# Moving one branch projection behind the next gate projection in a two-layer hybrid decoder on one Trainium2 core

## The chip, the cores and the metric

The kernel runs on one core of a Trainium2 chip. The metric is the device time of one execution in microseconds (us). The engines are named as the profile names them: PE is TensorE (PEld its weight loads), DVE is VectorE, ACT is ScalarE, POOL is GpSimd, and SP is SyncE, whose queue (SPq) issues the weight transfers.

## The reference: what is computed

Two layers (`DEPTH = 2`) of a decoder work on 256 tokens of width 1024, in float32. A layer is a token mixer and a SwiGLU, each followed by a LayerNorm. The mixer has three branches that read the same x: A is gated linear attention, B is retention, C is dilated window attention. Each branch gives 512 columns, is projected to 1024 columns, and is weighted by a sigmoid gate of its own:

```python
proj = x @ w_in
(gq, gk, gv, gr, ga, rq, rk, rv, rg, dq, dk, dv, gate) = jnp.split(proj, IN_SPLITS, axis=-1)
...
o_b = _retention_chunked(q_r, k_r, rv.reshape(B, S, N_HEADS, RET_DV))
o_b = _head_group_norm(o_b, ret_norm_g) * jax.nn.silu(rg.astype(F32))
...
y_a = o_a.astype(x.dtype) @ w_branch[0]
y_b = o_b.astype(x.dtype) @ w_branch[1]
y_c = o_c.astype(x.dtype) @ w_branch[2]
gates = jax.nn.sigmoid((gate + b_gate).astype(F32)).reshape(B, S, N_BRANCH, D_MODEL).astype(x.dtype)
merged = gates[:, :, 0] * y_a + gates[:, :, 1] * y_b + gates[:, :, 2] * y_c
return merged @ w_out
```

## The kernel before

**Numbers as two parts.** Every matrix operand is held as a high and a low part, and a product is three matmuls: high by high, low by high, high by low. For a weight, ACT (sometimes DVE, as a CAST) copies the staged block to the high part (`make_hi`, line 196), and DVE subtracts to get the low part (`make_lo`, line 215).

**Weights as a stream.** All weights come as units of 128 by 1024 in the order of use (512 KB each), through six staging buffers. The transfer of a unit is issued when the low part of the unit six places earlier has been made, because that frees its staging buffer. High and low parts live in a ring of 24 blocks (`NR = 24`, tile names `r`), which also holds other things; during the merge at most seven units are held at once (`state["cap"] = (NR - 10) // 2`, line 997). `take(n)` hands out the next units of the stream, `touch(u)` makes sure that both parts are there, and `free(u)` gives the two blocks back.

**The order of the work.** The program is written out by one pass of Python, with each engine's instructions in the order in which they are issued. Attention work runs in generators (`spawn`), which are advanced by one step at each `tick()` between matmul groups, so that it is woven into the dense projections. `await_((l, key))` (line 272) ticks until a generator has issued its last instruction; it is not a wait on the chip, which is done by semaphores.

**The merge (lines 997 to 1040).** For each quarter d of the output columns (256 columns) there are first three gate projections, each of two units and 48 matmuls (`a_pair`, line 408), each followed by a tanh on ACT. Then come three branch projections of one unit and 24 matmuls each, in the order C (`oc`), A (`oa`), B (`ob`). DVE multiplies each by its gate and adds it to the sum `mg`, and ACT and DVE split `mg` into the two parts of `MM`, which the output projection reads after all four quarters.

**What the branch projection reads.** `head_out` (line 871) closes a branch's generator: it transposes the branch's result on PE and lets ACT write the high part `OH` and DVE the low part `OL`, one head of 256 columns at a time. For the retention, `ret_all` (line 767) is issued last of the three; its group norm and its gate run on DVE and POOL before `head_out`.

Matmuls are recorded at line 130, transposes at line 134, ACT, DVE and POOL operations at line 118, and weight transfers at line 138. Rows name tiles without their buffer numbers: `xh`, `xl` are the two parts of x, `r` is a ring block, `pm` and `px` are PSUM banks, `f` are float32 blocks, and `stage` is a staging buffer.

Of the kernel before, what the change touches and what calls it, by code (L numbers as in the profile page):

```python
# [11 lines left out]
AF = mybir.ActivationFunctionType  # L12
OP = mybir.AluOpType
# [41 lines left out]
def trunk(ctx: ExitStack, tc: tile.TileContext, wst, xt_in, x_in, cst, tri, pcol, wga, wa2, lnp, out):  # L55
# [5 lines left out]
    def T(shape, tag, bufs=1, dt=F32):  # L61
        return sb.tile(shape, dt, tag=tag, name=tag, bufs=bufs)
# [11 lines left out]
    def when(log, ap, e):  # L74

        name, a, b = span(ap)
        return max([t + (e != "P" and OWN if by == e else HOP) for x, y, t, by in log.get(name, ()) if x < b and a < y], default=0.0)
# [43 lines left out]
    V = Timed(nc.vector, "V", 1.04, 65)  # L121
    A = Timed(nc.scalar, "A", 0.833, 110)
    G = Timed(nc.gpsimd, "G", 2.1, 450)
    act = A.activation
    stt = V.scalar_tensor_tensor
    ts = V.tensor_scalar

    def mm(out, lhsT, rhs, **k):
        issue("P", [out], [lhsT, rhs], size(out) * (4 if lhsT.dtype == F32 else 1) / 2.4 + 3)
        return nc.tensor.matmul(out, lhsT, rhs, **k)  # L130
# [37 lines left out]
    R = Blocks(sb, NR, 1024, "r", F32R)  # L168
    F4 = Blocks(sb, N4, 1040, "f4")
    F2 = Blocks(sb, N2, 512, "f2")  # L170
    PM = Blocks(psp, 3, 512, "pm")
# [3 lines left out]
    state = {"dma": 0, "made": 0, "whole": 0, "calm": False, "touched": 0, "freed": 0, "cap": NR // 2}  # L175
# [17 lines left out]
    def can_make():  # L193
        return state["made"] - state["freed"] < state["cap"] and len(R.free) >= 2

    def make_hi():
        u = state["made"]
        while state["dma"] <= u:
            dma_next()
        src = staged[u]  # L200
        hi, lo = parts[u] = R.free.pop(0), R.free.pop(0)
        if u in (2, 4, 6):
            start_split(u // 2 + 1)
        for c in halves(u):
            if u == 0:
                start_split(c.start // 512)
            if clk["A"] > clk["V"] + SWITCH:
                V.tensor_copy(hi[:, c], src[:, c])
            else:
                act(hi[:, c], src[:, c], AF.Copy)  # L210
            if u == 0:
                stt(lo[:, c], src[:, c], 1.0, hi[:, c].bitcast(F32), op0=OP.mult, op1=OP.subtract)
        state["made"] += 1

    def make_lo():
        u = state["whole"]
        src = staged.pop(u)
        hi, lo = parts[u]
        for c in halves(u) if u else ():
            stt(lo[:, c], src[:, c], 1.0, hi[:, c].bitcast(F32), op0=OP.mult, op1=OP.subtract)  # L220
        state["whole"] += 1
        if state["dma"] < u + 1 + STAGE:
            dma_next()

    def touch(u):
        state["touched"] = max(state["touched"], u + 1)
        n = 0
        while state["whole"] <= u:
            if state["whole"] < state["made"]:
                make_lo()  # L230
            elif len(R.free) >= 2:
                make_hi()
            else:
                tick()
                n += 1
                assert n < 2000, "ring"
        return parts[u]

    def free(u):
        assert u == state["freed"]  # L240
        R.put(*parts.pop(u))
        state["freed"] += 1

# [6 lines left out]
    def tick():  # L250
        for g in list(side):
            try:
                next(g)
            except StopIteration:
                side.remove(g)

        need = state["touched"] + 2
        late = clk["P"] + (CALM if state["calm"] else BACKLOG)
        if state["whole"] < state["made"]:
            hi = parts[state["whole"]][0]  # L260
            if state["whole"] < need or max(clk["V"], when(written, hi, "V")) < late:
                make_lo()
        if state["made"] < min(total, state["touched"] + AHEAD, state["whole"] + 2) and can_make():
            u = state["made"]
            there = u in staged and when(written, staged[u], "A") < clk["P"] + READY
            if u < need or there and min(clk["A"], clk["V"] - SWITCH) < late:
                make_hi()

    done = set()
    OT = {}  # L270

    def await_(*keys):
        left = 3000
        while not all(k in done for k in keys):
            tick()
            left -= 1
            assert left, keys
# [51 lines left out]
    hcol = T([128, L, 32], "hcol")  # L329
# [68 lines left out]
    def b_group(units, lh, ll, tt, ps, dl=1, last=False):  # L398

        n = len(units)  # L400
        for i, u in enumerate(units):
            b_unit(u, i, n, lh, ll, tt, ps, dl)
            if last:
                free(u)
            if i < n - 1:
                tick()

    def a_pair(units, rh, rl, ps):

        n = len(units)  # L410
        for a in range(2):
            for i, u in enumerate(units):
                hi, lo = touch(u)
                for j in range(4):
                    k = 4 * i + j
                    c0 = j * 256 + a * 128
                    o = ps[:, a * 256:a * 256 + 256]
                    mm(o, hi[:, c0:c0 + 128], rh(k), start=(i == 0 and j == 0), stop=False)
                    mm(o, hi[:, c0:c0 + 128], rl(k), start=False, stop=False)
                    mm(o, lo[:, c0:c0 + 128], rh(k), start=False, stop=(i == n - 1 and j == 3))  # L420
                if a == 1:
                    free(u)
                if not (a == 1 and i == n - 1):
                    tick()
# [3 lines left out]
    def take(n):  # L428
        r = list(range(base[0], base[0] + n))
        base[0] += n  # L430
        return r
# [466 lines left out]
    for l in range(L):  # L898
# [34 lines left out]
        us = take(8)  # L933
# [26 lines left out]
        for g in range(3):  # L960
# [3 lines left out]
            for which in range(2):  # L964
                for hp in range(2):
                    us = take(2)
                    ps = PM.main()[0]
# [28 lines left out]

        state["cap"] = (NR - 10) // 2
        MM = []
        for d in range(4):
            tg = []  # L1000
            for br in range(3):
                us = take(2)
                ps = PM.main()[0]
                a_pair(us, xh, xl, ps)
                t = F2.main()[0]
                for a in range(2):
                    c = br * 8 + d * 2 + a
                    act(t[:, a * 256:a * 256 + 256], ps[:, a * 256:a * 256 + 256], AF.Tanh,
                        bias=hcol[:, l, c:c + 1], scale=0.5)
                PM.put(ps)  # L1010
                tg.append(t)
                tick()
            mg = F2.main()[0]
            for br, key in ((2, "oc"), (0, "oa"), (1, "ob")):
                await_((l, key))
                OH, OL = OT[l, key]
                us = take(1)
                ps = PM.main()[0]
                a_pair(us, lambda k: OH[:, k * 256:k * 256 + 256], lambda k: OL[:, k * 256:k * 256 + 256], ps)
                if br == 2:  # L1020
                    stt(mg, tg[br], 1.0, ps, op0=OP.add, op1=OP.mult)
                else:
                    stt(tg[br], tg[br], 1.0, ps, op0=OP.add, op1=OP.mult)
                    V.tensor_add(mg, mg, tg[br])
                PM.put(ps)
                F2.put(tg[br])
                tick()
                if d == 3:
                    R.put(OH, OL)
            if d % 2 == 0:  # L1030
                MM.append(R.main(2))
            c = slice((d % 2) * 512, (d % 2) * 512 + 512)
            mh = MM[-1][0][:, c]
            act(mh, mg, AF.Copy, scale=0.5)
            stt(MM[-1][1][:, c], mg, 0.5, mh.bitcast(F32), op0=OP.mult, op1=OP.subtract)
            F2.put(mg)


        state["cap"] = (NR - 4) // 2
        ln1 = ln_params(l, 0)  # L1040
        us = take(8)
        for tt in range(2):
            st = T([128, 2, 6], "lnst", 2)
            for c in range(2):
                ps = PM.main()[0]
# [74 lines left out]
        for p in range(NPAIR):  # L1120
# [3 lines left out]
            t = F2.main()[0]  # L1124
# [199 lines left out]
```

## Time and profile before

| | |
|---|---|
| median of 3 runs | 1059.21 us (1058.38 to 1059.3) |
| the profiled execution's own time | 1059.59 us |
| its span (first to last instruction) | 1057.8 us |
| PE busy, share of the span | 1040.2 us, 98% |
| PEld / DVE / ACT / POOL busy | 954.2 / 695.7 / 485.5 / 17.9 us |
| mean granted TensorE clock | 0.995 of full speed |
| moved by DMA | 192.25 MB, 182 GB/s on the mean |

Busy times overlap, since the engines run side by side. A matmul's recorded duration overlaps with the next one's, so that a stretch of matmuls is measured from start to start. [...]

### The profile page before, as it was taken

What the parts mean: (1) busy time and instruction counts of PE and PEld (TensorE: products, weight loads), DVE (VectorE), ACT (ScalarE), POOL (GpSimd) and SP (SyncE); (2) the same over time, 40 slices, a digit from 0 to 9 for tenths busy, and PEclk for the clock granted to TensorE, in tenths of its full rate; (3) what the DMA queues carried; (4) which work ended last, traced back from release to release, by engine and by line L of the source; (5) the groups of instructions that cost most, each with busy time, mean ns of one, the idle gap of its engine ahead of it and who ended that gap; (6) DMA issues with size and microseconds to landing.
All of it is one profiled execution on the core that took longest, in us unless ns stands there. A gap on an engine that the chain in (4) does not pass through costs nothing.

```text
span 1057.8 us, 17494 instructions
## 1 busy us (share of the span) xinstructions
PE 1040.2 (98%) x7122; PEld 954.2 (90%) x7122; DVE 695.7 (66%) x1066; ACT 485.5 (46%) x733; POOL 17.9 (2%) x24
## 2 busy tenths in 40 slices
PE   8999999999999999999999999999899999999997
PEld 6999988898998899999889999878899988999996
DVE  6687765775658755454688767477666686555454
ACT  6565554543444444344364554654433545444330
POOL 0000000000000000000000000000000000000000
PEclk9999999999999999999999999999999999999999
DMA  9686633445666675555376456344456667665521
GB/s 340 231 276 196 204 114 123 141 140 187 191 173 216 191 257 180 192 195 190 120 275 201 143 167 204 106 134 139 131 178 192 193 197 248 206 199 176 192 91 40
DMA packets 55666, 192.25 MB, mean 182 GB/s; under 512 B 6257, under 2 KB 7409, under 8 KB 55586
## 3 DMA queue, kind: packets, MB, share of 16 engines
q1 hardware_dynamic: 50400, 180.38, 52.2%
q10 hardware_dynamic: 5186, 10.76, 3.1%
q8 instruction: 56, 0.92, 0.4%
q14 instruction: 24, 0.20, 0.1%
HBM read 187.93 MB, written 3.18 MB: 181 GB/s over the span
## 4 chain that ended last, share of the span: by engine, by line
PE 94%; DVE 3%; DMA 1%; POOL 1%; issue 1%; ACT 0%; SPq 0%; DVEq 0%
PE pm L130 75%; PE px L130 17%; PE px L134 2%; DVE r L118 1%; DVE f L118 1%; DMA stage<-in_wst_dram 1%; POOL rrs L118 0%; DVE rst L118 0%; ACT r L118 0%; SPq L138 0%; DVE xres L118 0%; POOL grs L118 0%; ACT junk L118 0%; DVE rmv L118 0%; DVE rve L118 0%
## 5 line engine op out<-in xcount | busy, mean ns | idle before, releaser
L130 PE MATMUL pm<-xh,r 128*128 128x256 f32 x2688 | 481.0, 280 | 0.0
L118 DVE SCALAR_TENSOR_TENSOR r<-stage,r 128x1024 fp32r<-128x1024 f32 (+1 forms) x341 | 402.0, 1215 | 50.9 <-ACT r L118 48.9
L130 PEld LDWEIGHTS pm<-xh,r 128*128 128x128 f32 x2688 | 414.1, 189 | 1.2
L118 ACT ACTIVATE r<-stage 128x1024 fp32r<-128x1024 f32 (+1 forms) x327 | 332.8, 1051 | 96.8 <-PE pm L130 35.0
L130 PE MATMUL pm<-xl,r 128*128 128x256 f32 x1344 | 375.3, 279 | 0.0
L130 PEld LDWEIGHTS pm<-xl,r 128*128 128x128 f32 x1344 | 253.2, 188 | 0.9
L130 PE MATMUL pm<-r,xh 128*128 128x512 f32 x672 | 214.9, 400 | 1.5 <-ACT r L118 0.9
L130 PEld LDWEIGHTS pm<-r,xh 128*128 128x128 f32 x672 | 123.5, 190 | 28.9 <-DVE r L118 1.8
L130 PE MATMUL pm<-r,xl 128*128 128x512 f32 x336 | 131.9, 393 | 0.0
L130 PE MATMUL pm<-r,r 128*128 128x256 f32 (+1 forms) x768 | 121.4, 317 | 6.5 <-DVE r L118 5.9
L130 PEld LDWEIGHTS pm<-r,r 128*128 128x128 f32 x768 | 108.8, 195 | 16.2 <-DVE r L118 8.1
L130 PE MATMUL px<-r,r 128*128 128x512 f32 x528 | 122.6, 389 | 0.0
L130 PEld LDWEIGHTS px<-r,r 128*128 128x128 f32 x528 | 97.9, 188 | 19.3
L118 DVE SCALAR_TENSOR_TENSOR f<-f,pm 128x512 f32<-128x512 f32 x52 | 35.7, 686 | 114.0 <-ACT f L118 93.7
L118 ACT ACTIVATE f<-pm 128x512 f32<-128x512 f32 x72 | 42.7, 594 | 141.9 <-PE pm L130 140.3
L130 PEld LDWEIGHTS pm<-r,xl 128*128 128x128 f32 x336 | 63.7, 190 | 13.8
L118 ACT ACTIVATE r<-f 128x512 fp32r<-128x512 f32 x28 | 17.7, 632 | 97.2 <-DVE f L118 97.2
L130 PE MATMUL px<-f,f 128*128 128x128 f32 (+4 forms) x368 | 47.4, 292 | 0.0
L130 PEld LDWEIGHTS px<-f,f 128*128 128x128 f32 (+2 forms) x368 | 42.7, 184 | 4.0 <-issue 0.7
L118 ACT ACTIVATE f<-px 128x512 f32<-128x512 f32 (+2 forms) x52 | 25.2, 506 | 41.2 <-PE px L130 29.2
L118 ACT ACTIVATE f<-pm,hcol 128x256 f32<-128x256 f32 x48 | 20.2, 474 | 51.1 <-PE pm L130 51.1
L118 DVE TENSOR_TENSOR f<-f,pm 128x512 f32<-128x512 f32 x22 | 15.1, 688 | 40.9 <-PE pm L130 40.7
(102 smaller groups left out, 485.9 us busy)
## 6 DMA issues: line engine op xcount, KB each, us to landing
stage<-in_wst_dram SPq DMA_DIRECT2D x339, 512.0 KB, 4.5
f<-in_lnp_dram ACTq DMA_DIRECT2D x8, 512.0 KB, 7.5
scr<-f ACTq DMA_DIRECT2D x8, 260.0 KB, 3.6
f<-scr ACTq DMA_DIRECT2D x4, 520.0 KB, 4.4
xres<-in_x_dram ACTq DMA_DIRECT2D x4, 256.0 KB, 5.5
out_dram<-xres SPq DMA_DIRECT2D x4, 256.0 KB, 2.0
f<-in_xt_dram SPq DMA_DIRECT2D x3, 256.0 KB, 8.6
cst<-in_cst_dram ACTq DMA_DIRECT2D x4, 192.0 KB, 3.2
```

Of the source, the lines that this page charges most:

```text
L118: return f(*a, **k)
L130: return nc.tensor.matmul(out, lhsT, rhs, **k)
L134: return nc.tensor.transpose(out, in_, ident)
```

## The change

In the first quarter (d = 0) of each layer, the retention's branch projection, its multiply and add, and the split of the first quarter's sum are no longer issued in their place. They are issued after the first gate projection of the second quarter (d = 1). The weight unit of the moved projection is still taken from the stream in its old place; two later units are given back before it, so the assertion that units come back in order is dropped.

```diff
     def free(u):
-        assert u == state["freed"]
         R.put(*parts.pop(u))
         state["freed"] += 1
...
+        late = None
+        for d in range(4):
+            tg = []
+            for br in range(3):
+                tg.append(merge_gate(d, br))
+                if late:
+                    branch(*late[1])
+                    merged(late[0], late[1][-1])
+                    late = None
+            mg = F2.main()[0]
+            for br, key in ((2, "oc"), (0, "oa"), (1, "ob")):
+                us = take(1)
+                if d == 0 and br == 1:
+                    late = d, (us, br, key, tg[br], mg)
+                else:
+                    branch(us, br, key, tg[br], mg)
+                if d == 3:
+                    R.put(*OT[l, key])
+            if not late:
+                merged(d, mg)
```

`merge_gate`, `branch` and `merged` hold the old loop's body, line by line.

The first place is PE in layer 0, at the end of the first quarter's projection of branch A (`r_83`, `r_84` are A's two parts, `r_82`, `r_73` its weights). Here `px_113<-cst,f_95` are the last four transposes of the retention's result, `r_76`, `r_77` are its `OH` and `OL`, `r_85`, `r_86` the weight unit of its projection, and `r_87`, `r_88`, `r_65`, `r_66` the two units of the next gate. Before:

```order
L130 MATMUL pm_107<-r_83,r_73 128x256
L134 MATMUL px_113<-cst,f_95 128x128 x4
L130 MATMUL pm_106<-r_76,r_85 128x256 [waits Activation_49]
L130 MATMUL pm_106<-r_77,r_85 128x256 [waits DVE_49]
L130 MATMUL pm_106<-r_76,r_86 128x256
...
L130 MATMUL pm_108<-xh,r_87 128x256
L130 MATMUL pm_108<-xl,r_87 128x256
L130 MATMUL pm_108<-xh,r_88 128x256
```

With the change:

```order
L134 MATMUL px_113<-cst,f_95 128x128 x4
L130 MATMUL pm_106<-xh,r_87 128x256 [waits Activation_49]
L130 MATMUL pm_106<-xl,r_87 128x256
L130 MATMUL pm_106<-xh,r_88 128x256
...
L130 MATMUL pm_106<-xh,r_66 128x256 [waits DVE_49]
...
L130 MATMUL pm_108<-r_76,r_85 128x256 [waits DVE_49,Activation_49]
L130 MATMUL pm_108<-r_77,r_85 128x256 [waits DVE_49]
L130 MATMUL pm_108<-r_76,r_86 128x256
```

The 24 matmuls of the retention's projection and the 48 of the gate have changed places; the transposes stand where they stood. Layer 1 shows the same exchange.

The second place is DVE in layer 0, from the split of the gate's second unit (`r_66`) on. `r_77<-px` are the low parts `OL`, two heads to a row, `f_105<-f_105,pm` is the multiply behind the retention's projection, and `r<-stage,r` are low parts of weight units. Before:

```order
L118 SCALAR_TENSOR_TENSOR r_66<-stage,r_65 128x1024 [waits DMAHW0_49,Activation_49]
...
L118 SCALAR_TENSOR_TENSOR r_77<-px_113,hcol,r_76 128x256 [waits Activation_49] x2
L118 SCALAR_TENSOR_TENSOR r_79<-stage,r_78 128x1024 [waits DMAHW4_49,Activation_49]
L118 SCALAR_TENSOR_TENSOR f_105<-f_105,pm_106 128x512 [waits PE_49]
L118 TENSOR_TENSOR f_102<-f_102,f_105 128x512 [waits DVE_49]
L118 SCALAR_TENSOR_TENSOR r_73<-f_102,r_82 128x512 [waits Activation_49]
L118 SCALAR_TENSOR_TENSOR r_81<-stage,r_80 128x1024 [waits DMAHW5_49]
L118 SCALAR_TENSOR_TENSOR r_86<-stage,r_85 128x1024 [waits DMAHW6_49,Activation_49]
```

With the change:

```order
L118 SCALAR_TENSOR_TENSOR r_66<-stage,r_65 128x1024 [waits DMAHW0_49,Activation_49]
...
L118 SCALAR_TENSOR_TENSOR r_77<-px_113,hcol,r_76 128x256 [waits Activation_49] x2
L118 SCALAR_TENSOR_TENSOR r_79<-stage,r_78 128x1024 [waits DMAHW4_49,Activation_49]
L118 SCALAR_TENSOR_TENSOR r_81<-stage,r_80 128x1024 [waits DMAHW5_49,Activation_49]
L118 SCALAR_TENSOR_TENSOR r_73<-stage,r_82 128x1024 [waits DMAHW6_49,Activation_49]
L118 SCALAR_TENSOR_TENSOR f_105<-f_105,pm_108 128x512 [waits PE_49]
L118 TENSOR_TENSOR f_102<-f_102,f_105 128x512 [waits DVE_49]
L118 SCALAR_TENSOR_TENSOR r_66<-f_102,r_65 128x512 [waits Activation_49]
```

Everything up to the last `OL` is as before; then two weight splits stand ahead of the multiply, the add and the split of the sum, where they stood behind them. On ACT, one weight copy per layer is added that was a CAST on DVE, and the rest keeps its kind and count; SP issues the same transfers in the same order.

## Rows read from the trace of the kernel before

**Rows 1.** The page's first part: busy time, share of the span, instructions.

```profile
PE 1040.2 (98%) x7122; PEld 954.2 (90%) x7122; DVE 695.7 (66%) x1066; ACT 485.5 (46%) x733; POOL 17.9 (2%) x24
```

**Rows 2.** The waits of PE: us in total, times, longest us.

```profile
PE pm L130 <- DVE r L118: 6.5, 6, 2.2
PE px L130 <- DVE f L118: 2.2, 3, 1.5
```

**Rows 3.** Timeline of PE, layer 0: start, us, what, idle before it.

```profile
235.30 0.36 PE L130 MATMUL pm<-r,r 128*128 128x256 f32 x1
236.44 1.64 PE L130 MATMUL pm<-r,r 128*128 128x256 f32 x6 [0.77 <-DVE r L118]
240.31 4.38 PE L130 MATMUL pm<-r,r 128*128 128x256 f32 x17 [2.23 <-DVE r L118]
244.50 0.38 PE L130 MATMUL pm<-xh,r 128*128 128x256 f32 x1
...
261.56 8.69 PE L130 MATMUL pm<-r,r 128*128 128x256 f32 x71
```

**Rows 4.** Timeline of PE, the same place in layer 1.

```profile
757.85 0.36 PE L130 MATMUL pm<-r,r 128*128 128x256 f32 x1
...
762.79 4.34 PE L130 MATMUL pm<-r,r 128*128 128x256 f32 x17 [2.23 <-DVE r L118]
766.97 0.28 PE L130 MATMUL pm<-xh,r 128*128 128x256 f32 x1
```

**Rows 5.** Windows, PE alone: length, PE busy (count), PEclk, DMA share, GB/s.

```profile
238.00:240.00 2.00, 0.08 (x1) 1.00 0.97 293
240.00:242.00 2.00, 1.54 (x6) 0.83 0.54 217
242.00:244.00 2.00, 2.00 (x11) 0.50 0.18 10
246.00:248.00 2.00, 2.00 (x19) 1.00 0.04 16
```

**Rows 6.** Timeline of DVE, layer 0.

```profile
231.90 3.49 DVE L118 SCALAR_TENSOR_TENSOR r<-stage,r 128x1024 fp32r<-128x1024 f32 x3
...
240.80 0.48 DVE L118 SCALAR_TENSOR_TENSOR r<-px,hcol,r 128x256 fp32r<-128x256 f32 x1 [0.54 <-ACT r L118]
241.75 1.23 DVE L118 SCALAR_TENSOR_TENSOR r<-stage,r 128x1024 fp32r<-128x1024 f32 x1 [0.46 <-ACT r L118]
244.74 0.69 DVE L118 SCALAR_TENSOR_TENSOR f<-f,pm 128x512 f32<-128x512 f32 x1 [1.76 <-PE pm L130]
...
247.52 2.35 DVE L118 SCALAR_TENSOR_TENSOR r<-stage,r 128x1024 fp32r<-128x1024 f32 x2
```

**Rows 7.** Timeline of DVE, layer 1.

```profile
754.39 3.49 DVE L118 SCALAR_TENSOR_TENSOR r<-stage,r 128x1024 fp32r<-128x1024 f32 x3
...
763.28 0.48 DVE L118 SCALAR_TENSOR_TENSOR r<-px,hcol,r 128x256 fp32r<-128x256 f32 x1 [0.54 <-ACT r L118]
```

**Rows 8.** Timeline of ACT, layer 0.

```profile
240.67 1.99 ACT L118 ACTIVATE r<-stage 128x1024 fp32r<-128x1024 f32 x2
...
250.46 0.84 ACT L118 ACTIVATE f<-pm,hcol 128x256 f32<-128x256 f32 x2 [2.62 <-PE pm L130]
...
256.11 0.84 ACT L118 ACTIVATE f<-pm,hcol 128x256 f32<-128x256 f32 x2 [2.92 <-PE pm L130]
```

**Rows 9.** A short stop of PE in layer 0 (timeline).

```profile
202.79 0.71 PE L130 MATMUL px<-f 64*128 64x128 f32 x6 [0.36 <-DVE f L118]
```

**Rows 10.** Window round the first stop: us; PE, PEld, DVE, ACT, POOL busy; PEclk, DMA, GB/s.

```profile
196.00:206.00 10.00, 9.64 (x72) 7.79 (x71) 5.08 (x13) 5.59 (x20) 2.03 (x2) 1.00 0.62 210
```

**Rows 11.** What the weight supply waits for: SPq and ACT, whole run.

```profile
SPq L138 <- DVE r L118: 847.4, 328, 15.5
...
ACT r L118 <- PE pm L130: 35.0, 26, 3.4
```

**Rows 12.** DMA issues: KB each, median us from issue to landing.

```profile
stage<-in_wst_dram SPq DMA_DIRECT2D x339, 512.0 KB, 4.5
```

More of the change, by code (lines that the diff above doesn't have):

```diff
@@ L998, in trunk, with merge_gate, branch, merged @@
         MM = []
[L999 to L1029, printed above, removed]
+        def merge_gate(d, br):
+            us = take(2)
+            ps = PM.main()[0]
+            a_pair(us, xh, xl, ps)
+            t = F2.main()[0]
+            for a in range(2):
+                c = br * 8 + d * 2 + a
+                act(t[:, a * 256:a * 256 + 256], ps[:, a * 256:a * 256 + 256], AF.Tanh,
+                    bias=hcol[:, l, c:c + 1], scale=0.5)
+            PM.put(ps)
+            tick()
+            return t
+        def branch(us, br, key, t, mg):
+            await_((l, key))
+            OH, OL = OT[l, key]
+            ps = PM.main()[0]
+            a_pair(us, lambda k: OH[:, k * 256:k * 256 + 256], lambda k: OL[:, k * 256:k * 256 + 256], ps)
+            if br == 2:
+                stt(mg, t, 1.0, ps, op0=OP.add, op1=OP.mult)
+            else:
+                stt(t, t, 1.0, ps, op0=OP.add, op1=OP.mult)
+                V.tensor_add(mg, mg, t)
+            PM.put(ps)
+            F2.put(t)
+            tick()
+        def merged(d, mg):
             if d % 2 == 0:
@@ L1036, in trunk @@
             F2.put(mg)
+        late = None
[12 more added lines that the diff above has]
+                    late = d, (us, br, key, tg[br], mg)
+                else:
+                    branch(us, br, key, tg[br], mg)
[3 more added lines that the diff above has]
+                merged(d, mg)
         state["cap"] = (NR - 4) // 2
```

## The prediction

> **What bounds the kernel now.** I read the page first. PE is busy for 98% of the span, DVE for 66% and ACT for 46% [rows 1], so only a stretch in which PE stands still, or runs slowly, can be worth anything. The second view is PE's own waits. They come to little: 6.5 us of matmuls behind DVE's writes to ring blocks in six waits, 2.2 us the longest, and 2.2 us in three waits at the attention's small products [rows 2]. The third view, PE's timeline, shows where the long ones lie. In layer 0 the first matmul of the retention's projection starts at 235.30. PE then stands still for 0.77 us, does six matmuls, stands still for 2.23 us, and does the other 17 in 4.38 us; the next gate starts at 244.50 [rows 3]. Layer 1 does the same from 757.85 to 766.97 [rows 4]. DVE's timeline says for what PE waits: the last of the retention's low parts (`OL`) is begun at 240.80 and lasts 0.48 us [rows 6], so it is there at 241.28; in layer 1 at 763.76 [rows 7]. DVE comes to them late because the retention's group norm runs through it and three weight splits stand ahead (231.90, 3.49 us) [rows 6].
>
> The windows add a second cost that the waits don't show. The granted clock is 1.00 while PE has almost nothing to do (238 to 240), 0.83 over the next two us, 0.50 from 242 to 244, where PE is busy all the time, and 1.00 again from 246 [rows 5]. [...] So the 17 matmuls after the stop run at half speed, and the stop costs more than its idle time.
>
> **What the stop costs.** The same work without a stop: the three branch projections of the second quarter are 72 matmuls in a row, of which 71 have records, from 261.56 for 8.69 us [rows 3]. Less the 0.2 us by which the last one's record outlasts the step to the next, that is 8.5 us, or 2.8 us for 24. In layer 0 they took 244.50 - 235.30 = 9.2 us, which loses 6.4 us; in layer 1 766.97 - 757.85 = 9.1 us, which loses 6.3 us [rows 3, 4]. Of the 6.4 us, 0.77 + 2.23 = 3.0 are idle; the last 17 take 244.50 - 240.31 = 4.2 us where 17 x 2.8/24 = 2.0 would do, so 2.2 are the slow clock; and the remaining 1.2 are the first seven matmuls, which take 0.36 + 1.64 us for 0.8, held up head by head.
>
> **The change part by part.** *Nothing is removed.* PE issues the same matmuls; 48 of the gate come ahead of 24 of the branch. The transposes that feed `OH` and `OL` stand where they stood, and DVE's order up to the last `OL` is word for word the same, so I let that last `OL` end at 241.28 and 763.76 as before. It waits for no matmul that is moved.
>
> *The gate moved forward.* Its length is the distance from one gate's tanh to the next in the second quarter: 256.11 - 250.46 = 5.65 us, or 0.118 us for each of its 48 matmuls [rows 8]. It would begin at 235.30 and end at 240.95. Does it have its weights? Its first unit was split before the retention's norm; the low part of its second unit is the first of the three splits at 231.90 and so is there at 233.1 [rows 6]. Its first use is the fifteenth matmul, 14 x 0.118 = 1.6 us behind the start, at 236.9: 3.8 us to spare. In layer 1 the split ends at 755.6 and the use is at 759.5 [rows 4, 7]. So the gate doesn't wait.
>
> *The branch moved back.* It starts at 240.95. Its heads come in order, and the last one's low part is read by the eleventh matmul, ten steps of 0.118 us later, at 242.1, against 241.28. That is 0.8 us to spare. In layer 1 it is 757.85 + 5.65 + 1.2 = 764.7 against 763.76, 0.9 us. So the wait is covered, but with a margin of under 1 us, and this is the tightest place of the forecast. With PE busy throughout, there is nothing left that would take the clock down here: the stretch from 196 to 206 holds a stop of 0.36 us, with the clock at 1.00 [rows 9, 10].
>
> *DVE and ACT behind it.* Two splits now stand ahead of the branch's multiply. The first of them follows the split at 241.75, which ends at 242.98 [rows 6]; its high part is the second ACT copy of the pair at 240.67, done at 242.66 [rows 8]. So it ends at 244.2. The second needs a high part that ACT can copy only after the gate's tanh (0.84 us) and its own 1.0 us, at 244.5, and ends at 245.7. The multiply then starts at 245.7 and not at the branch's end, 243.8. Its PSUM bank is wanted next by the second quarter's first branch projection, at 240.95 + 2.8 + 2 x 5.65 = 255.05: nine us of cover, so I cost the 1.9 us at nothing; without that cover it would cost 1.9 us per layer. The split of the sum is read by the output projection alone, after three more quarters. The CAST that becomes an ACT copy takes 1.05 us per layer on an engine that is 46% busy. The weight transfers keep their order and number.
>
> **The sum.** 1059.59 - 6.4 - 6.3 = 1046.9 us for an execution like the profiled one, which lies 0.4 us above the runs' median. I say 1046.7.
>
> **Rivals.**
>
> *The wait only becomes shorter.* If DVE's chain ends x us later than before, PE waits x - 0.8 us. For it speaks the small margin, and that DVE then works beside a PE that is busy rather than idle. Against it, the operations in question have waits on ACT and POOL, none on moved work. Nothing in the rows gives x. Its bounds are 0 and the 2.23 us of the old stop; at 2.2 the wait is 1.4 us, and if the clock falls again another 2.2 us at most, 3.6 us per layer: 1047 to 1054 us. Still faster.
>
> *PE runs ahead and finds its weights late, so that the gain is given back.* PE comes 6.4 us earlier to everything behind. The second quarter's first branch unit has its low part at 248.7 (two splits from 247.52) and is used at 261.56, a lead of 12.9 us [rows 3, 6]. After the change I have 244.2 against 255.05, a lead of 10.8. Against it: SPq spends 847 us in 328 waits for DVE's splits, and ACT waits 35 us for PE to release blocks, so the stream stands at its ring's limit and not at the memory's [rows 11]. The likeliest place for a late unit is the second of the two splits that now stand ahead of the multiply: while it waits for its transfer, so do the multiply and everything behind it on DVE. A unit takes 4.5 us to land [rows 12], and this one's transfer is issued when the first of the splits at 231.90 ends, at 233.1, so it lands near 238, and ACT wants it at 243.5: it would have to be 11 us later still before PE's next branch, at 255.05, waited. [...] If part or all of the lead were lost, the time would be anything from 1047 up to 1059.6.
>
> *The ring runs dry and the kernel is slower.* The old order gave the branch's unit back at its end, one after the other. Now it is held for a gate longer (5.65 us), with at most seven units in the ring. If a new unit can only start when one comes back, each costs a transfer (4.5 us), a copy (1.0) and a split (1.2) in a row, 6.7 us, where PE uses one in 2.8 us: 3.9 us lost per unit. It decides against the change from the point at which the lead of 10.8 us is used up; from then on two late units per layer lose 7.8 us and more than eat the 6.4 us, and at three the time is 1059.6 - 12.7 + 6 x 3.9 = 1070 us. Against it speaks that the gate ahead gives two units back at 240.95, 3 us before the held one comes due.
>
> That the change doesn't do what it says is excluded by the order of PE's rows: the swap is there in both layers, and nowhere else.
>
> **How the numbers follow.** I give the forecast 0.86, the shortened wait 0.06, the weights running late 0.05 (of which 0.02 within 0.2% of before) and the ring 0.03. 0.2% (2 us) is about what a measurement of this kernel can tell from no change. So faster is 0.86 + 0.06 + 0.03 = 0.95, same 0.02, slower 0.03. For the range I take the likeliest case and part of the first rival. PE's other waits in the old kernel, 2.2 us at the small products [rows 2], are the most that a shifted order could also take away, so the low end is 1045.0; the upper end leaves room for a rest wait of 1 us per layer, 1049.0. Beyond it lie most of the first rival and the other two, 0.12 together.
>
> **What would show it right or wrong.** Right: PE's waits behind DVE's ring blocks fall from 6.5 us to under 1; the granted clock stays at 1.00 between 235 and 250; the gate starts near 235.3 and the branch takes 2.8 us from about 241; the second gate starts near 243.8 and its rest is 6.4 us earlier than before, and 12.7 us earlier behind layer 1's merge. DVE's multiply starts near 245.7, with no one waiting. Wrong: a stop of PE at the branch's seventh to eleventh matmul with a clock of 0.50 behind it (the first rival), or PE waiting for `r<-stage` at the later gates (the other two). The span would tell the rest: a shortened merge but an unchanged span would mean that the gain is given back in the feed-forward part.

## The result, and the profile after

The changed kernel's median is 1046.89 us (four runs, 1044.9 to 1048.09) against 1059.26 us (four runs, 1058.38 to 1059.53): a ratio of 0.9883 with a 95% interval of 0.9865 to 0.99. 1046.7 us was forecast. The profiled execution took 1048.09 us, with a span of 1046.2 us.

The page's first part after the change answers to [rows 1]:

```profile
PE 1034.1 (99%) x7122; PEld 950.7 (91%) x7122; DVE 693.9 (66%) x1064; ACT 487.2 (47%) x735; POOL 17.9 (2%) x24
```

PE's waits answer to [rows 2] (us in total, times, longest us):

```profile
PE pm L130 <- ACT r L118: 2.4, 1, 2.4
PE px L130 <- DVE f L118: 2.2, 3, 1.5
```

The line of 6.5 us behind DVE's ring blocks is gone. PE's busy time is 6.1 us shorter although it does the same matmuls; a part of that is the half clock: in the windows, 11 matmuls are busy for 2 us at 0.50 [rows 5] and 19 at 1.00 (below). In the list there is now one wait of 2.4 us for ACT, which lies elsewhere (below). The timeline of PE in layer 0, which answers to [rows 3]:

```profile
237.57 0.60 PE L134 MATMUL px<-cst,f 128*128 128x128 f32 x4
237.92 0.36 PE L130 MATMUL pm<-xh,r 128*128 128x256 f32 x1
...
243.66 3.04 PE L130 MATMUL pm<-r,r 128*128 128x256 f32 x24
246.54 0.28 PE L130 MATMUL pm<-xh,r 128*128 128x256 f32 x1
```

The gate follows the transposes at once and lasts 5.74 us; the retention's projection follows without a stop and takes 2.88 us. From the gate's start to the next gate's start are 8.62 us. Before, the projection began at 235.30 [rows 3], and the next gate but one, whose first matmul is the second of this row, began at 250.25:

```profile
250.14 0.40 PE L130 MATMUL pm<-xh,r 128*128 128x256 f32 x2
```

That is 14.95 us for the same 72 matmuls, so the change saves 6.33 us here. In layer 1 the same stretch takes 8.61 us instead of 14.78 us and saves 6.17 us. The windows, which answer to [rows 5], show the granted clock (PEclk) in shares of full speed:

```profile
240.00:242.00 2.00, 2.00 (x19) 1.00 0.96 326
242.00:244.00 2.00, 2.00 (x19) 1.00 0.78 229
```

DVE in the same place, as in [rows 6]:

```profile
243.43 0.49 DVE L118 SCALAR_TENSOR_TENSOR r<-px,hcol,r 128x256 fp32r<-128x256 f32 x1 [0.54 <-ACT r L118]
244.38 2.36 DVE L118 SCALAR_TENSOR_TENSOR r<-stage,r 128x1024 fp32r<-128x1024 f32 x2 [0.46 <-ACT r L118]
247.00 1.23 DVE L118 SCALAR_TENSOR_TENSOR r<-stage,r 128x1024 fp32r<-128x1024 f32 x1 [0.26 <-ACT r L118]
248.14 0.68 DVE L118 SCALAR_TENSOR_TENSOR f<-f,pm 128x512 f32<-128x512 f32 x1
```

The whole program stands 2.62 us later here than before (237.92 against 235.30). Less that, the last low part is begun at 240.81 (240.80 before) and the multiply at 245.5 (245.7 was forecast): up to the last low part DVE has not moved, PE has.

A measure that leaves the rest of the program out is the distance on ACT from the tanh behind the first quarter's third gate to the tanh behind the third quarter's first gate, with the same matmuls in between in both kernels. Below it is called *the distance*. Before, in layer 0, it is 275.86 - 228.98 = 46.88 us:

```profile
228.98 0.84 ACT L118 ACTIVATE f<-pm,hcol 128x256 f32<-128x256 f32 x2 [5.40 <-PE pm L130]
...
275.86 0.84 ACT L118 ACTIVATE f<-pm,hcol 128x256 f32<-128x256 f32 x2 [2.42 <-PE pm L130]
```

After, it is 271.72 - 231.60 = 40.12 us:

```profile
231.60 0.84 ACT L118 ACTIVATE f<-pm,hcol 128x256 f32<-128x256 f32 x2 [5.40 <-PE pm L130]
...
271.72 0.84 ACT L118 ACTIVATE f<-pm,hcol 128x256 f32<-128x256 f32 x2 [2.43 <-PE pm L130]
```

Layer 1 has 46.71 and 40.11 us. So the two merges are 6.76 and 6.60 us shorter, 13.4 us in sum: 12.5 us at the old stop, and 0.43 us per layer in the second and third gates of the second quarter, which took 5.65 us each before [rows 8] and take 5.44 us now. The spans differ by 1057.8 - 1046.2 = 11.6 us. The rest lies in two other places. 2.62 us are lost in the first 60 us of this execution, 1.8 of them in the first 16 us. And layer 1's first stretch gains 0.8 us. -13.36 + 2.62 - 0.83 = -11.57. Two of these pieces stand in the chain of work (start, us, engine and line, matmuls). Before:

```profile
30.07 30.18 PE pm L130 x228
536.64 44.75 PE pm L130 x288
```

After:

```profile
31.86 31.01 PE pm L130 x228
532.51 43.94 PE pm L130 x288
```

The same 228 matmuls lose 0.83 us and the same 288 gain 0.81 us, without a wait. In both kernels three matmuls of 256 columns took 340 or 353 ns from start to start (the last experiments), and these two stretches and the two gates changed from the one to the other.

### The profile page after: what moved, and what is told of

Read it like the earlier page. It is cut to its first block, busy times and chain, and to the rows that moved or that the text cites. A ratio compares the mean times of both kernels' runs of the same rounds, so it can differ in the third digit from the quotient of the medians.

```text
span 1046.2 us, 17496 instructions
## 1 busy us (share of the span) xinstructions
PE 1034.1 (99%) x7122; PEld 950.7 (91%) x7122; DVE 693.9 (66%) x1064; ACT 487.2 (47%) x735; POOL 17.9 (2%) x24
## 4 chain that ended last, share of the span: by engine, by line
PE 98%; DMA 1%; DVE 1%; issue 0%; ACT 0%; POOL 0%; SPq 0%; DVEq 0%
PE pm L130 78%; PE px L130 18%; PE px L134 2%; DMA stage<-in_wst_dram 1%; DVE xres L118 0%; POOL grs L118 0%; DVE f L118 0%; ACT junk L118 0%; SPq L138 0%; DVE lnst L118 0%; DVEq L1338 0%; ACT r L118 0%; DVE gss L118 0%; DVE mv L118 0%; DVE ve L118 0%
## 5 line engine op out<-in xcount | busy, mean ns | idle before, releaser
L118 ACT ACTIVATE r<-stage 128x1024 fp32r<-128x1024 f32 (+1 forms) x329 | 334.8, 1052 | 96.6 <-PE pm L130 39.9
L130 PE MATMUL pm<-r,r 128*128 128x256 f32 (+1 forms) x768 | 115.2, 310 | 0.0
L130 PEld LDWEIGHTS pm<-r,r 128*128 128x128 f32 x768 | 105.3, 190 | 7.3
```

Of the source, the lines that this page charges most:

```text
L118: return f(*a, **k)
```

## The experiments

Times and ratios are against the kernel before in the same series. Two theories are told apart throughout. Mine is that PE stopped, once per layer, for the retention's late low parts, that the stop took the clock down too, and that one gate covers it whole. Against it stand the rivals of the forecast (a margin that doesn't hold, weights that come late, a ring that runs dry) and that the gain is something of the whole program.

**The change in one layer (layer0).**

```diff
-                if d == 0 and br == 1:
+                if l == 0 and d == 0 and br == 1:
                     late = d, (us, br, key, tg[br], mg)
```

> The change in layer 0 alone, layer 1 as before. My theory (a stop of TensorE that is the same in each layer is taken away): layer 0's merge is shortened by the 6.8 us that the changed kernel shows there, layer 1's stop from its retention projection stays at 9.1 us with the clock at 0.50 behind it; time 1059.2 - 6.8 = 1052.4 us, ratio about 0.9935. Rival (the gain is one of the whole program, by the order in which ring blocks come back): layer 1 gains too, or layer 0 gains another amount than 6.8 us.

1052.0 us, ratio 0.9935 (0.9919 to 0.995). The distance is 40.12 us in layer 0 and 46.83 us in layer 1. Layer 1's timeline of PE still has the stop:

```profile
750.76 1.65 PE L130 MATMUL pm<-r,r 128*128 128x256 f32 x6 [0.73 <-DVE r L118]
754.64 4.39 PE L130 MATMUL pm<-r,r 128*128 128x256 f32 x17 [2.23 <-DVE r L118]
```

The second idle time is that of [rows 4]; the first was 0.71 us in the kernel before:

```profile
758.92 1.64 PE L130 MATMUL pm<-r,r 128*128 128x256 f32 x6 [0.71 <-DVE r L118]
```

The gain is local, and half of it belongs to each layer. That layer 1 is as long as before hides two differences that nearly cancel. The half clock lasts longer here and reaches into the next gate, which starts at 758.83:

```profile
758.00:760.00 2.00, 2.00 (x11) 0.50 0.82 231
```

And the second and third gates take 5.44 us each instead of 5.65 us, although this layer has PE's old order.

**The splits behind the low parts, PE's order as before (hold).** The flag is set in `ret_all` behind the last gate multiply, and cleared at the end of `head_out`.

```diff
+            state["hold"] = tt == 1
...
+        state["hold"] = False
...
-        if state["whole"] < state["made"]:
+        if state["whole"] < state["made"] and not state["hold"]:
             hi = parts[state["whole"]][0]
```

> TensorE's order as before; instead no weight split is issued on VectorE between the retention's last gate multiply and its last low part, so that the splits that stood ahead of the low parts stand behind them. My theory (the low parts were late because VectorE had 3.5 us of splits and one more of 1.2 us ahead of them): the last low part comes at about 238.5 instead of 241.3, TensorE stops for about 2 us instead of 3, in two pieces, and the projection takes 5 us instead of 9.2 if the clock stays up, 6.5 if it falls; time 1050.5 to 1054. Rival (the low parts wait for the group norm and the transposes, and the splits only fill its gaps): the projection still takes 8 us or more; time 1057 or more.

1051.58 us, ratio 0.9929 (0.9904 to 0.9955). The distance is 41.94 us in layer 0 and 43.50 us in layer 1. PE's timeline, layer 0 and then layer 1:

```profile
237.88 1.19 PE L130 MATMUL pm<-r,r 128*128 128x256 f32 x7
240.08 2.96 PE L130 MATMUL pm<-r,r 128*128 128x256 f32 x17 [1.01 <-DVE r L118]
242.88 0.29 PE L130 MATMUL pm<-xh,r 128*128 128x256 f32 x1
...
754.65 1.20 PE L130 MATMUL pm<-r,r 128*128 128x256 f32 x7
756.86 3.96 PE L130 MATMUL pm<-r,r 128*128 128x256 f32 x17 [1.01 <-DVE r L118]
760.62 0.41 PE L130 MATMUL pm<-xh,r 128*128 128x256 f32 x1
```

The projection took 5.0 us in layer 0, as expected with the clock up. The last low part is begun 9.01 us behind the tanh instead of 11.82 us. So the splits in DVE's order were what made the low parts late: with them moved, half of the gain and more comes without touching PE's order. Layer 1 shows the same stop, to the hundredth, and yet 17 matmuls that take 1.0 us longer. The windows say why:

```profile
240.00:242.00 2.00, 1.77 (x10) 1.00 0.00 0
242.00:244.00 2.00, 2.00 (x19) 1.00 0.34 74
...
758.00:760.00 2.00, 2.00 (x12) 0.61 0.07 4
760.00:762.00 2.00, 2.00 (x11) 0.54 0.92 264
```

The same stop of 1.01 us left the clock at 1.00 in the one layer and was followed by windows at 0.61 and 0.54 in the other. Layer 0 also tells what the half clock cost in the kernel before: its last 17 matmuls take 242.88 - 240.08 = 2.8 us at a clock of 1.00, still held up by the last low part, where the old ones took 4.2 us [rows 3]. That is 1.4 us.

**Filling the stop with work that is thrown away (fill).**

```diff
                 ps = PM.main()[0]
+                if d == 0 and br == 1:
+                    for _ in range(36):
+                        mm(ps[:, 0:256], touch(us[0])[0][:, 0:128], xh(0), start=True, stop=True)
```

> TensorE's order as before, with 36 matmuls of 256 columns added ahead of the first quarter's retention projection in each layer; their sums are thrown away. They take 36 x 0.1175 = 4.2 us, which is nearly the stop. My theory (of the 6.4 us lost per layer some 2 are the half clock that the stop brings): the clock stays at 1.00, the last low part still comes at 241.3, the projection ends near 243.1 instead of 244.5; time 1059.2 - 2 x 1.4 = 1056.4 us. Rival (the clock's fall is not brought by the stop, or costs nothing): the projection ends at 244.5 or later as before, time 1059.2 or more.

1055.42 us, ratio 0.9962 (0.9949 to 0.9975), a little better than expected. The distances are 44.76 and 44.73 us, 2.1 and 2.0 us shorter than before.

```profile
236.85 4.49 PE L130 MATMUL pm<-xh,r 128*128 128x256 f32 x36
241.17 3.66 PE L130 MATMUL pm<-r,r 128*128 128x256 f32 x24
244.67 0.29 PE L130 MATMUL pm<-xh,r 128*128 128x256 f32 x1
```

The kernel stands 1.55 us later here than before (230.53 against 228.98 at the tanh), so the projection ends at 243.1 in the old kernel's time, not at 244.5. The clock is 1.00 in every window from 234 to 248. A kernel with 72 matmuls more is faster: the half clock behind the stop is a cost of its own, 1.4 us here, as in hold, and it is gone with the 36 matmuls in the stop. The other 0.7 us per layer are the three gates behind it, which go faster (below).

**Behind two gates instead of one (two_gates).**

```diff
-                if late:
+                if late and br == 1:
                     branch(*late[1])
```

> As the changed kernel, but the retention's projection stands behind two gates of the second quarter instead of one. My theory (one gate covers the wait whole, with 0.8 us to spare): no further gain, 1046.9 us within 1.5 us. Rival (the margin is too small in some executions, or the cover is not whole): 1 us or more faster than the changed kernel; or, if holding the unit longer starves the ring, slower.

1046.6 us, ratio 0.9878 (0.9861 to 0.9895), the same as the changed kernel's. The distances are 40.34 and 40.32 us, 0.2 us longer; the two gates ahead of the projection take 11.39 us together, so the second of them has not gone to the faster step. One gate (5.74 us) was cover enough, and holding the unit for another gate cost no more than these 0.2 us per layer.

**The retention's low parts made later (late1, late4, late8).** The same edit with 1, 4 and 8 operations, on the changed kernel:

```diff
+            if key == "ob" and hp == 0:
+                for _ in range(4):
+                    nc.vector.scalar_tensor_tensor(OL[:, 0:512], o[:, 0:512], 1.0, o[:, 512:1024],
+                                                   op0=OP.mult, op1=OP.subtract)
             if col is None:
```

> As the changed kernel, with one more VectorE operation of 0.7 us ahead of the retention's first low part in each layer (it writes values that are overwritten). My theory (0.8 us of margin): still no stop at the projection; from the tanh behind the first quarter's third gate to the tanh behind the third quarter's first gate 40.1 us, as in the changed kernel. Rival (no margin, each delay of VectorE comes through): 40.8 us.

> As the changed kernel, with four such operations (2.8 us) ahead of the retention's first low part in each layer. My theory (0.8 us of margin): TensorE stops for about 2.0 us in all at the projection; the same distance is 42.1 us if the clock stays at 1.00, up to 44.3 if it falls to half. Rival (more margin than I think, or none): 40.1, or 42.9 us and more with the clock at 1.00.

> As the changed kernel, with eight such operations (5.5 us) ahead of the retention's first low part in each layer. My theory: a stop of about 4.7 us, the clock falls to 0.50 behind it, and the distance is 45 to 47 us, nearly the 46.9 us of the kernel before. Rival (the clock does not fall, since TensorE was busy up to the stop): 44.8 us with the clock at 1.00.

Measured, with the distance in us (the start of the last low part is counted from the same tanh, 11.83 us in the changed kernel):

| | last low part later by | distance, layers 0 and 1 | more than the changed kernel | lowest granted clock in the merge |
|---|---|---|---|---|
| changed kernel | - | 40.12, 40.11 | - | 1.00 |
| late1 | 0.80 | 40.13, 40.12 | 0.01 | 1.00 |
| late4 | 2.99 | 42.31, 42.25 | 2.2 | 1.00 |
| late8 | 5.89 | 47.65, 47.40 | 7.5, 7.3 | 0.50 |

late4's last low part is begun at 243.16, 14.82 us behind its tanh at 228.34; late8's at 247.07, 17.72 us behind 229.35; late1's 12.63 us behind its tanh. So late1 is free and late4 costs 2.2 us of its 3.0: the margin is 0.8 us, as forecast. late8 would cost 5.9 - 0.8 = 5.1 us by the wait alone, and costs 2.4 us more (2.2 us in layer 1). Its timeline of PE in layer 0, and behind it the windows:

```profile
242.71 1.65 PE L130 MATMUL pm<-r,r 128*128 128x256 f32 x6 [1.01 <-DVE r L118]
246.59 4.38 PE L130 MATMUL pm<-r,r 128*128 128x256 f32 x17 [2.23 <-DVE r L118]
```

```profile
248.00:250.00 2.00, 2.00 (x11) 0.50 0.03 8
250.00:252.00 2.00, 2.00 (x11) 0.50 0.73 231
252.00:254.00 2.00, 2.00 (x16) 0.75 0.97 324
```

This is the old stop, moved behind the gate: the same 17 matmuls in 4.38 us. Here the half clock outlasts them by some 2 us and slows the next gate too, which is why it costs more than the 1.4 us of the kernel before. late4's timeline has a stop too, but in its windows the clock stays at 1.00:

```profile
242.67 2.97 PE L130 MATMUL pm<-r,r 128*128 128x256 f32 x17 [1.27 <-DVE r L118]
```

```profile
242.00:244.00 2.00, 1.19 (x5) 1.00 0.87 250
244.00:246.00 2.00, 2.00 (x19) 1.00 0.03 8
```

**The changed kernel once more (again).** No edit.

> The changed kernel once more, in more rounds: its four times lay between 1044.9 and 1048.1 us. My theory (the spread comes from the first 50 us, where the profiled execution lost 2.6 us that the change has nothing to do with): the time stays near 1046.5 us, and an execution without that loss in its first 50 us spans about 1043.5 us. Rival (the spread comes from the merge, where the margin is under 1 us): a slower execution shows a stop at the retention's projection.

1045.84 us (1044.89 to 1045.96), ratio 0.9862 (0.9838 to 0.9886). The profiled execution spans 1044.1 us and has the distance 40.12 us in both layers, with the clock at 1.00 from 228 to 248. The first tanh of the measure is at 229.47 instead of 231.60. So the 2.1 us by which the two profiled executions differ arose before the merge. In the first changed execution the timeline of PE and the window of the first 15 us say where 1.3 us of it arose:

```profile
8.59 1.52 PE L130 MATMUL pm<-r,xh 128*128 128x512 f32 x2 [2.40 <-ACT r L118]
```

```profile
0.00:15.00 15.00, 11.09 (x38) 0.89 0.82 286
```

A wait for the first split weights (2.4 us), and a clock of 0.89 over this window. The repeat's first 15 us have a clock of 1.00, and the other 0.8 us are the stretch of 228 matmuls, which goes at the faster step again:

```profile
0.00:15.00 15.00, 11.74 (x43) 1.00 0.83 294
```

```profile
30.56 30.18 PE pm L130 x228
```

No stop at the retention's projection is in either, so the margin has no part in the difference of these two; the other executions have no profile.

**The step of the matmuls (probe, short, short64, short_dil).** The traces showed that three matmuls of 256 columns take either 340 or 353 ns from start to start, mostly one or the other for a whole gate. The feed-forward pairs behind the first of each layer go at 353 before and after. The probe put another number and width of thrown-away matmuls ahead of each:

```diff
             pg = PM.main()[0]
+            w, n = FILL[l].get(p, (0, 0))
+            for _ in range(n):
+                mm(pg[:, 0:w], touch(ug[0])[0][:, 0:128], xh(0)[:, 0:w], start=True, stop=True)
             a_pair(ug, xh, xl, pg)
```

> About the two step times of TensorE that the traces show (three matmuls of 256 columns in 340 or 353 ns, the one or the other for a whole gate). The changed kernel, with one to sixteen short matmuls (16 to 256 columns, thrown away) ahead of each gate projection of the feed-forward part, of another kind in each of the fourteen places. Guess (what runs just ahead of a projection sets its step): behind some kinds the 96 matmuls of a pair take 10.9 us instead of 11.3 us, which would be worth 0.4 us for each pair. Rival (the step hangs on the tiles or on the code's place): all stay at 353 ns and the kernel is slower by the 2 to 4 us that the added matmuls take.

1048.01 us in the one execution. Behind one matmul of 64, 96 or 192 columns, two or eight of 128, and four, eight or sixteen of 64 the pair went at 340 ns; behind one of 16, 32, 128 or 256, two of 256 and four of 128 at 353. Each kind was tried once. Then one matmul of 64 columns ahead of seven pairs in each layer:

```diff
+            if 0 < p < NPAIR - 1:
+                mm(pg[0:128, 0:64], touch(ug[0])[0][:, 0:128], xh(0)[:, 0:64], start=True, stop=True)
             a_pair(ug, xh, xl, pg)
```

> The changed kernel with one matmul of 64 columns (thrown away) ahead of the first gate projection of each feed-forward pair but the first and the last, seven per layer. In the run before this one a matmul of 64 columns brought the pair's 96 matmuls from 353 to 340 ns per three, and cost about 0.13 us itself. Theory (the short matmul sets the step): 14 x (32 x 13.3 ns - 0.13 us) = 4.1 us less than the changed kernel, near 1042 us. Rival (the step fell in that run by its mixture of kinds): the pairs stay at 353 ns and the time is 1046 to 1048 us.

1042.64 us (five runs, 1041.63 to 1043.89), ratio 0.9837 (0.9823 to 0.985). In the chain of work, whose lines are start, us, engine and line with a count, a pair takes 11.02 us in this kernel, with its 97th matmul:

```profile
383.70 11.02 PE pm L130 x97
482.55 21.90 PE pm L130 x193
```

and 11.31 us in the changed kernel without it:

```profile
384.43 11.31 PE pm L130 x96
484.91 22.61 PE pm L130 x192
```

Twelve of the fourteen stand alone and save 0.29 us each, as expected. The last of each layer runs on into a pair without a short matmul of its own, which goes faster too: 0.71 us for both. That is 4.9 us in sum, where 4.1 us were expected; against the two medians of the changed kernel from other series, 1046.89 and 1045.84 us, the kernel gains 4.2 and 3.2 us. The same with weights of 64 columns (`hi[:, 0:64]`, and 64 rows of the sum) in place of 128:

> As the run with a matmul of 64 columns ahead of each pair, but its weights are 64 columns wide too. Theory (only the moving columns matter for the step, and the narrower weights load faster): as fast as that run or up to 0.8 us faster, near 1041.5 us. Rival (the width of the weights sets the step): the pairs stay at 353 ns, 1046 to 1048 us.

1047.78 us, ratio 0.9885 (0.9871 to 0.9898): all pairs stay at 353 ns.

```profile
381.30 11.42 PE pm L130 x97
```

That falsifies the guess that only the moving columns matter: the medians of the two runs, in one series, lie 5.1 us apart. Whether the narrower weights loaded faster here was not shown; in the kernel before, loads of 16 columns (`px<-xh,gah`) took 94 ns on the mean and loads of 128 (`pm<-xh,r`) 189 ns. The last run added one short matmul ahead of the first query projection of each dilated group (`if which == hp == 0`):

> As the run with a matmul of 64 columns ahead of each feed-forward pair, and one more ahead of the first query projection of each of the three dilated groups of both layers, six in all. Theory (each of these stretches of 192 matmuls goes at 340 ns too): where they went at 353 ns, the 32 threes behind the third group gain 0.4 us each and the others up to 0.8 us, less 0.13 us each: 0 to 2 us faster than with the feed-forward ones alone. Rival (transposes and attention matmuls in between set the step anew, or these stretches are fast already): no gain, or 0.8 us slower by the six matmuls.

1042.61 us (1041.62 to 1043.24), ratio 0.9837 (0.9823 to 0.985): no gain over the feed-forward ones alone, as its rival had it. One stretch even goes the other way. With the short matmul ahead, layer 1's dilated stretch takes

```profile
529.07 44.87 PE pm L130 x289
```

and without it, in the run before,

```profile
529.45 43.93 PE pm L130 x288
```

So the matmul of 64 columns did not bring the faster step there.

## Why the prediction was right

*What bounds the kernel:* right. The stop was the one thing of weight in PE's waits, and taking it away in one layer gave one layer's share (layer0).

*What the stop costs:* right. I put it at 6.4 and 6.3 us; over the 72 matmuls that changed places the kernel saves 6.33 and 6.17 us. The distance falls by 6.76 and 6.60 us. The rest, 0.43 us per layer, I did not see: the second and third gates of the second quarter had run at 353 ns per three matmuls in the old kernel's trace (5.65 us each [rows 8]) and run at 340 ns in the new one's, 5.44 us from tanh to tanh. Taking 5.65 us as the length of a gate that doesn't change was a mis-sized term. The exchange alone doesn't explain it: layers with PE's old order have 5.44 us too, in hold, in fill and in layer 1 of layer0. Why the kernel before had 5.65 us in its one profile is open.

*That the half clock is part of the cost:* right in kind, too large. Filling the stop with useless work gives 1.4 us per layer back, and hold's layer 0, with the clock up, does the last 17 matmuls 1.4 us faster. The forecast put 2.2 us on the clock; 0.8 us of that were the heads of these 17, which waited for the last low part whatever the clock. The sum is the same, since both parts went with the stop. In late8 the clock's fall adds 2.4 us, because it lasts longer there.

*That DVE's chain would not move:* right to 0.01 us. Why it was late (splits ahead of the low parts) is shown by hold.

*The margin of 0.8 us:* right; late1 is covered, late4 shows 0.8 us of cover. It is the tightest place of the forecast, but it held in both profiled executions of the changed kernel.

*The two splits ahead of the multiply cost nothing:* right. The multiply came at 245.5 in the old kernel's time, and PE did not wait. In both traces DVE's operations stand in the order of issue: before, it was idle for 1.76 us ahead of the multiply [rows 6], with the next split's high part there since 242.66 [rows 8]; after, the second split waited 0.26 us for its copy, and the multiply came behind it. two_gates delays the multiply by a whole gate more and costs 0.2 us, in a gate's step. The 11 us by which the forecast let the second split's unit be late left out the copy and the split behind it; the nine us of cover that it named for the multiply are the bound, and neither was used.

*The rivals:* no run here shows the weights running late or the ring running dry: PE waits for no staged unit at the merge, and ACT waits longer for PE to release blocks than before (39.9 us against 35.0 [rows 11]). The shortened wait exists, but only once DVE is pushed back by more than 0.8 us (late1 by 0.80 us: no stop; late4 by 2.99 us: 1.27 us at the last 17 matmuls).

*The sum:* 12.7 us were forecast, the medians differ by 12.4 us, and the spans by 11.6 us. The stop itself gives 12.5 us, so the forecast is right for its own reason. That the medians agree to 0.3 us is partly luck: the gates behind the stop give 0.9 us and layer 1's first stretch 0.8 us more, and this execution's start took 2.6 us back. The kernel before varies more still in a later series (1057.5 to 1062.61 us); why the start varies was not tried.

## What to carry to other kernels

Look in the waits for the matmul that stands at the head of a busy engine with data of another engine's last step, and put work that is ready in front of it; its length has to exceed the lateness (here a gate of 5.74 us, which left 0.8 us to spare), and the profile gives both to a tenth of a microsecond. Read the granted clock behind a stop of TensorE in the windows, and count slow matmuls there as part of the stop's cost (here 1.4 us per layer at 0.50); the list of waits does not show them. Compare them with the same matmuls at full clock behind the same wait, or what is still waiting is put down to the clock (here 0.8 of 2.2 us). Before exchanging the order on the waiting engine, look also at the late engine's order: here four weight splits ahead of the last small operations were worth more than half of the gain.

## What the runs showed of the hardware that was not expected

- The clock's fall did not go by the stop's length alone. In one execution (hold) the same stop of 1.01 us, behind the same seven matmuls in 1.2 us, left the clock at 1.00 in layer 0 and was followed by 0.61 and 0.54 in layer 1, which cost 1.0 us in the 17 matmuls behind it and 1.6 us in the distance. A stop of 1.27 us in late4 left it at 1.00; pairs of stops, 0.7 to 1.0 us and 2.23 us six matmuls later, took it to 0.50 each time (the kernel before, layer 1 of layer0, late8). What decides it is open.
- Streams of 256-column matmuls kept one of two steps at a granted clock of 1.00: 340 ns or 353 ns for three. In the feed-forward pairs it went by what stands just ahead: one matmul of 64 columns with 128 columns of weights brought feed-forward pairs from 11.31 to 11.02 us with itself, and the kernel to 0.9837 of the time before, faster than both kernels. With 64 columns of weights, or (in one try each) with 16, 32, 128 or 256 moving columns, it did not. Ahead of layer 1's dilated stretch the same matmul did not bring the faster step either, and one stretch of 228 matmuls took 31.01 us in one execution of the changed kernel and 30.18 us in the next. What sets the step is not settled.
